# Two-layer encoder trunk on one core: the large loads move from SyncE's DMA queue to ScalarE's, and the planner gets two queues

## The chip, the cores and the metric

One core of one Trainium2 chip. The metric is device time in microseconds of one execution; lower is better. Before the change it is 1849.16 us, the median of three runs (1848.88 to 1854.86).

## What is computed

Two token groups (512 and 1024 rows, D = 1024) go through the same two layers. Cut to what matters:

```python
def even_layer(x, ...):                       # layer 0
    h = rms_norm(x, norm_g)
    qa, ka, va, qb, kb, vb, gate = split(h @ w_in)
    oa = gqa_attention(rope(norm(qa)), rope(norm(ka)), va)          # "A": 8 heads
    ob = diff_attention(rope(norm(qb)), rope(norm(kb)), vb, lam)    # "B": 4 heads, p0 - lam * p1
    mix = concat(oa, norm(ob)) * silu(gate)
    return x + mix @ w_out

def odd_layer(x, ...):                        # layer 1
    q, k, v, gate = split(rms_norm(x, norm_g) @ w_in)
    o = dilated_attention(q, k, v)            # "C": three (window, dilation) patterns, 16 heads
    return x + (o * silu(gate)) @ w_out
```

## The kernel before

**Precision by splitting.** Every matmul of a projection, of probabilities with V, and of the output is done in fp16 on split operands: ScalarE writes the high half (`f_hi`), VectorE the rest (`f_lo`), and TensorE makes three passes (`PASSES`, line 35). So each piece of data runs through ScalarE, VectorE, a transposing DMA and TensorE.

**Order of the work.** The program is cut into stages (`Plan.add`, line 66). A stage has an engine, a duration that the author estimates, dependencies, and buffers ("tokens") that it takes and gives back. `Plan.run` (line 96) plays the stages against these durations as a list scheduler: each engine takes the first stage by position whose inputs are ready and whose buffers are free, and emits its instructions there and then. So the durations decide the order in which instructions stand on each engine; on the chip every engine then runs its own list in order and waits at semaphores.

**DMAs in the planner.** `Plan.dma` (line 85) makes three stages of a transfer: an issue on SP (0.6 us for an ordinary one), a stage on one shared "DMA" server that works first come first served, and a latency. `tdma` (line 92) does it for a transposing DMA: with 2048 columns SP is taken for 0.05 + 2048 x 0.975e-3 us in the plan. All DMAs are issued from SP (`nc.sync`).

**What is loaded.** Large loads are 512 KB tiles of f32: two gain vectors (`norm_gain`, line 301), 12 token tiles in layer 0 (`l0_h`, line 1539), 74 blocks of weights (`wprep`, line 415: two for each pair of column blocks), and in `out_tile` for each of 24 output tiles the gated mix (line 1269) and the residual (lines 1302, 1306, 1307, 1309; 26 issues, as the first tile of each group in layer 1 takes two). These are 138 issues. Most of them land in the six f32 buffers `f4`, which attention uses as well for its exponentials.

**What is transposed.** `transp` (line 359, called from `t_av` and `out_tile`) turns a [128, 2048] fp16 tile of probabilities or of the mix; line 386 does it for the normalised tokens `hT`; line 594 turns queries and keys (1024 columns). TensorE's products with V (line 784) and the output projections (line 492 with `t`) cannot start before the transposed tile has landed.

**Stages in time.** Start and first projections to about 110 us; attention A with its projections to 450; B to 760; output of layer 0 and first projections of layer 1 to 1010; C to 1690; output of layer 1 to the end.

Of the kernel before, what the change touches and what calls it, by code (L numbers as in the profile page):

```python
# [20 lines left out]
D = 1024  # L21
# [20 lines left out]
LAG = {"PE": 0.25, "SP": 0.0, "DMA": 0.0, "LAT": 0.05, "ACT": 0.2, "DVE": 0.15, "POOL": 0.17}  # L42
LAT0 = 0.75


class Stage:
    def __init__(self, eng, dur, fn, pos, seq):
        self.eng, self.dur, self.fn, self.pos, self.seq = eng, dur, fn, pos, seq
        self.nd, self.succ, self.acq, self.rel = 0, [], [], []
        self.ready, self.done = 0.0, None  # L50
# [9 lines left out]
class Plan:  # L60
    def __init__(self, caps):
        self.caps = dict(caps)
        self.stages = []
        self.pos = 0.0

# [19 lines left out]
    def dma(self, issue, dur, fn, deps=(), acq=(), use=(), pos=None, keep=0, tail=1.25):  # L85


        a = self.add("SP", issue, fn, deps, acq, use, pos, keep)
        x = self.add("DMA", dur, None, [a], (), tuple(acq) + tuple(use), pos)
        return self.add("LAT", tail, None, [x], (), tuple(acq) + tuple(use), pos)  # L90

    def tdma(self, cols, *args, **kw):

        return self.dma(0.05 + cols * 0.975e-3, cols * 0.9e-3, *args, tail=1.2 + cols * 0.25e-3, **kw)

    def run(self):
# [17 lines left out]
        while n < len(self.stages):  # L114
            progress = False
            for e, q in engs.items():
# [24 lines left out]
                heapq.heappush(events, (now + s.dur, 1, s.seq, s))  # L141
                if e == "SP":
                    heapq.heappush(events, (now + LAT0, 2, s.seq, s))
# [8 lines left out]
            while events and events[0][0] <= now + 1e-9:  # L152
                t, kind, _, s = heapq.heappop(events)
                if kind == 0:
                    heapq.heappush(engs[s.eng], (t if s.eng == "DMA" else s.pos, s.seq, s))
                elif kind == 2:
                    release(s, t)
                else:
                    busy[s.eng] = False
                    s.done = t  # L160
                    for tok in s.rel:
                        tok.users -= 1
                        if tok.users == 0:
                            free[tok.kind].append(tok.slot)
                    if s.eng != "SP":
                        release(s, t)
# [3 lines left out]
def pe(n, cnt):  # L170
    return cnt * (n / 2400.0 + 0.0027)
# [34 lines left out]
T_ROW = dict(dur=1.3, tail=1.9)  # L206
T_COL = dict(dur=1.75, tail=1.9)
# [6 lines left out]
def trunk_kernel(ctx: ExitStack, tc: tile.TileContext, A: dict, outs: list):  # L214
    nc = tc.nc
# [76 lines left out]
    def norm_gain(l, deps=()):  # L292
# [5 lines left out]
        def f_ld():  # L298
            v = new(tok).rearrange("p a b c -> p (a b c)")
            b["g"], b["junk"] = v[:, 0:2048].bitcast(F32), v[:, 2048:3072].bitcast(BF16)  # L300
            nc.sync.dma_start(out=b["g"], in_=A[f"norm{l}"].unsqueeze(0).to_broadcast([128, D]))
# [97 lines left out]
    def wprep(w, cols, ih=None, iz=None, kinds=("whl",), deps=(), keep=2):  # L399
# [117 lines left out]
    def qk_stages(zb, ztok, evs, e2, tabs, tdep, ti, kind, isq, dst, dst_acq, dst_use, swap, dst_dep=()):  # L517
# [43 lines left out]
        else:  # L561
# [19 lines left out]
            s = add("DVE", dve(512) + 2 * dve(64) + 2 * dve(128) + 0.3 + (dve(384) if isq else 0.0), f_rope, [sr, tdep], [s1t],  # L581
# [484 lines left out]
    def att_C(u, gi):  # L1066
# [73 lines left out]
        def send():  # L1140
# [4 lines left out]
            s = add("ACT", act(512) + 0.12, f_ev, avs23[-1:], [pkt], [ot23])  # L1145
# [115 lines left out]
    def out_tile(l, g, tl, wo, mix_deps, x_deps, finish):  # L1261
# [36 lines left out]
        def f_x():  # L1298
            x = b["x"] = new(xt)
            if l == 0:  # L1300
                src = A["x_prompt"] if g == 0 else A["x_sample"]
                nc.sync.dma_start(out=x, in_=src[0, 128 * tl:128 * tl + 128, :])
            else:
                base = GROWS[g]
                if tl == 0:
                    nc.sync.dma_start(out=x[0:64, :], in_=x1buf[base + n - 64:base + n, :])
                    nc.sync.dma_start(out=x[64:128, :], in_=x1buf[base:base + 64, :])
                else:
                    nc.sync.dma_start(out=x, in_=x1buf[row - 64:row + 64, :])
        sx = dma(ISSUE, fn=f_x, deps=[x_deps, sl], acq=[xt], keep=1, **T_ROW)  # L1310
        evs, mms = [], []
        for hf in range(2):
# [21 lines left out]
            evs.append(add("DVE", 2 * dve(256) + 0.25, f_ev, [m, sx, evs], (), [pt, xt]))  # L1334
# [191 lines left out]
    def l0_h(g, tls, kinds):  # L1526
# [4 lines left out]
        for i, tl in enumerate(tls):  # L1531
            t1t = Token("t1")

            def f_ld(i=i, tl=tl):
# [4 lines left out]
                nc.sync.dma_start(out=b[i], in_=src[0, 128 * tl:128 * tl + 128, :])  # L1539
# [177 lines left out]
```

## Time and profile before

| | us |
|---|---|
| median of three runs | 1849.16 |
| the profiled execution's own time | 1854.62 |
| span in its trace (first to last instruction) | 1852.4 |
| TensorE (PE) busy | 1675.0 |
| VectorE (DVE) busy | 1332.2 |
| ScalarE (ACT) busy | 1212.8 |
| GpSimd (POOL) busy | 695.5 |

TensorE is busy in 90% of the span, so the time that it idles is the first thing to look at. Issues of DMAs are not in the busy times: SP has no busy time on the page, and an issue on another engine would show as idle time of that engine. How long SP is held by an issue stands in the timeline, in rows that begin with SPq.

### The profile page before, as it was taken

Reading aid. Unit: us, or ns where it says so; the run is one execution under the profiler, and the core shown is the slowest. Engines: PE = TensorE matmul, PEld = TensorE weight load, DVE = VectorE, ACT = ScalarE, POOL = GpSimd, SP = SyncE. Lnnn points to the kernel's source line nnn. Section 1 sums busy time; section 2 is a strip of 40 time slices with the busy share of each in tenths; the row PEclk is TensorE's granted clock in tenths of the full one; section 3 lists DMA queues with packets and bytes.
Section 4 is the critical chain, followed back from the end, with each engine's and each line's share of the span. In section 5 each row is a group of like instructions: output and inputs, shape, how many; then the busy total and the mean of one; then the engine's idle time right before and its main releaser. Section 6 shows DMA issues by size and latency. Waiting matters only on the chain. (4 is left out here: it accounts for less than half of the span.)

```text
span 1852.4 us, 44798 instructions
## 1 busy us (share of the span) xinstructions
PE 1675.0 (90%) x17626; PEld 1398.4 (75%) x17626; DVE 1332.2 (72%) x2985; ACT 1212.8 (65%) x2593; POOL 695.5 (38%) x1204
## 2 busy tenths in 40 slices
PE   4898978989999999699898999999999999995898
PEld 3776756878887878378787887888788888774788
DVE  7788878767888778965635778677777777787332
ACT  6488978767777767853425676678676757777220
POOL 6523333333463445312212344354444444452200
PEclk9999999999999999799899999999999999996999
DMA  9989999795565445689975676676766757776983
GB/s 251 191 157 166 182 177 167 146 163 113 98 125 101 109 92 122 147 198 224 207 176 128 122 150 131 138 143 140 147 132 144 137 116 151 148 145 140 232 230 103
DMA packets 788724, 282.06 MB, mean 152 GB/s; under 512 B 647072, under 2 KB 772256, under 8 KB 788512
## 3 DMA queue, kind: packets, MB, share of 16 engines
q1 hardware_dynamic: 788512, 279.19, 73.4%
q8 instruction: 138, 2.26, 0.5%
q14 instruction: 74, 0.61, 0.1%
HBM read 73.92 MB, written 25.17 MB: 53 GB/s over the span
## 5 line engine op out<-in xcount | busy, mean ns | idle before, releaser
L492 PE MATMUL pj<-whl,hT 128*128 128x256 f16 x7680 | 882.3, 275 | 22.2 <-DMA hT<-h 21.2
L492 PEld LDWEIGHTS <-hT 128*128 128x128 f16 x7968 | 782.8, 99 | 145.6 <-DMA hT<-h 23.1
L784 PEld LDWEIGHTS <-t 128*128 128x128 f16 x4992 | 200.5, 100 | 93.8 <-DMA t<-h 85.8
L1107 ACT ACTIVATE f<-f,cs,csc 128x256 f32<-128x256 f32 (+1 forms) x384 | 218.4, 570 | 65.5 <-DVE cs L778 65.4
L492 PEld LDWEIGHTS <-t 128*128 128x128 f16 x2304 | 228.9, 100 | 40.0 <-DMA t<-h 9.8
L800 DVE TENSOR_TENSOR h<-f,h 128x1024 f16<-128x1024 f32 x148 | 187.7, 1273 | 57.4 <-ACT h L796 55.0
L784 PE MATMUL pj<-V,t 128*128 128x64 f16 (+1 forms) x4032 | 178.7, 204 | 51.2 <-DMA t<-h 47.8
L492 PE MATMUL pj<-whl,t 128*128 128x256 f16 x1728 | 202.4, 279 | 8.2 <-DMA t<-h 8.2
L772 PE MATMUL S<-K,q 128*128 128x512 f16 x640 | 169.6, 399 | 33.3 <-ACT f L1024 19.1
L796 ACT ACTIVATE h<-f 128x1024 f16<-128x1024 f32 x168 | 175.5, 1051 | 21.9 <-DMA t<-h 19.8
L535 POOL TENSOR_SCALAR qs<-qs,we 128x8 f32<-128x8 f32 x87 | 44.5, 511 | 354.0 <-DVE qs L529 343.1
L261 POOL TENSOR_TENSOR qs<-qs,mhalf 128x8 f32<-128x8 f32 x87 | 147.8, 1699 | 7.3
L772 PEld LDWEIGHTS <-q 128*128 128x128 f16 x640 | 61.0, 101 | 91.7 <-issue 42.8
L854 DVE TENSOR_REDUCE as<-S 128x1 f32<-128x1024 f32 (+1 forms) x80 | 95.9, 1219 | 29.1 <-PE S L772 28.9
L423 ACT ACTIVATE t<-f 128x1024 bf16<-128x1024 f32 x74 | 77.8, 1051 | 44.5 <-DMA f<-in_w_in_dram 32.6
L864 ACT ACTIVATE f<-S,as,asc 128x1024 f32<-128x1024 f32 (+1 forms) x96 | 101.7, 1061 | 4.0 <-DVE h L800 0.5
L478 DVE SCALAR_TENSOR_TENSOR whl<-f,wsm,whl 128x1024 f16<-128x1024 f32 x68 | 87.7, 1305 | 8.2 <-ACT whl L473 8.2
L1332 DVE SCALAR_TENSOR_TENSOR f<-pj,os,f 128x256 f32<-128x256 f32 x96 | 41.9, 479 | 68.0 <-PE pj L492 61.2
L1018 DVE TENSOR_REDUCE bs<-S 128x1 f32<-128x1024 f32 x64 | 77.2, 1217 | 16.2 <-PE S L772 16.2
L800 POOL TENSOR_TENSOR h<-f,h 128x1024 f16<-128x1024 f32 x20 | 43.5, 2175 | 120.9 <-ACT h L796 120.9
L473 ACT ACTIVATE whl<-f,wsm 128x1024 f16<-128x1024 f32 x68 | 75.8, 1140 | 16.8 <-PE pj L492 14.3
L1122 PE MATMUL S<-K,q 128*128 128x256 f16 (+1 forms) x384 | 79.3, 371 | 4.6 <-DVE m L1097 4.6
(250 smaller groups left out, 2684.5 us busy)
## 6 DMA issues: line engine op xcount, KB each, us to landing
f<-in_w_in_dram SPq DMA_DIRECT2D x58, 512.0 KB, 5.3
mixbuf<-sg SPq DMA_DIRECT2D x48, 256.0 KB, 2.8
f<-mixbuf SPq DMA_DIRECT2D x24, 512.0 KB, 5.7
K<-K SPq DMA_DIRECT2D x78, 128.0 KB, 2.5
f<-in_w_out_dram SPq DMA_DIRECT2D x16, 512.0 KB, 4.5
pn<-pk SPq DMA_DIRECT2D x96, 66.0 KB, 2.2
x1buf<-f SPq DMA_DIRECT2D x12, 512.0 KB, 4.1
Vc<-V SPq DMA_DIRECT2D x96, 64.0 KB, 2.3
```

What stands on the lines that cost most here:

```text
L261: G.tensor_tensor(y, v, mhalf[:, 0:n], ALU.pow)
L423: S_.activation(out=junk1(t1t), in_=b[i].rearrange("p k n -> p (k n)"), func=AF.Square, accum_out=b["s"][:, i:i + 1])
L478: stt(out=part(k, 1, i), in0=b[i][:, nk * k:nk * k + nk, :], scalar=sc(), in1=part(k, 0, i), op0=M, op1=SU)
L492: T.matmul(ps, lhs(k, a), wt(k, b), start=(k == 0 and i == 0), stop=(k == 7 and i == 2))
L772: T.matmul(out[:, 512 * i:512 * i + 512], q, u.K[:, st, gi, hk, :], start=(st == 0), stop=(st == 1))
L784: T.matmul(o, t4[:, 8 * a + base + k, :], v(k, b), start=(k == 0 and i == 0), stop=(k == nk - 1 and i == 2))
L796: S_.activation(out=b["hl"][:, 0, :], in_=b["e"], func=AF.Copy)
L800: (G if on_pool else V).tensor_tensor(b["hl"][:, 1, :], b["e"], b["hl"][:, 0, :], SU)
L854: V.tensor_reduce(out=b["s"][:, 0:nh], in_=b["S"].rearrange("p (h k) -> p h k", h=nh), op=ALU.max, axis=AX.X)
L864: S_.activation(out=b["e"][:, w * i:w * i + w], in_=b["S"][:, w * i:w * i + w], func=AF.Exp, bias=b["s"][:, 2 + i:3 + i], scale=u.sc, accu ...
L1107: S_.activation(out=b["e"][:, w * i:w * i + w], in_=b["e"][:, w * i:w * i + w], func=AF.Exp, bias=b["s"][:, i:i + 1], scale=u.sc, accum_ou ...
L1122: T.matmul(s[:, L * i:L * i + L], q, k, start=(sk == 0), stop=(sk == 1))
```

## The change

The 138 loads named above are issued from ScalarE (`nc.scalar.dma_start`). Everything else stays on SP: transposing DMAs, the swapped copies of K (lines 599, 600), Vc, pn, the spills of the mix, the stores of results, and the small tables.

The planner learns of it. A transfer is now an issue on its own queue ("SP" or "ACT") and a landing that `transfer` works out when the issue is placed. For each queue it keeps when its last transfer was served and landed. An ordinary issue holds its engine for 0.6 us. A transposing one holds it for 0.6 + 0.64e-3 us per column, or until what is ahead of it on the same queue has nearly landed, whichever is longer. Transfers of the two queues don't delay each other in this model. Some durations are raised: matmuls by 2%, a rotary stage of queries by 0.25, the eviction of an output tile by 0.25, the copy of a C tile by 0.28 us.

```diff
-LAG = {"PE": 0.25, "SP": 0.0, "DMA": 0.0, "LAT": 0.05, "ACT": 0.2, "DVE": 0.15, "POOL": 0.17}
+LAG = {"PE": 0.25, "SP": 0.0, "LAT": 0.05, "ACT": 0.2, "DVE": 0.15, "POOL": 0.17}
...
+        self.served, self.landed = {"SP": 0.0, "ACT": 0.0}, {"SP": 0.0, "ACT": 0.0}
...
-    def dma(self, issue, dur, fn, deps=(), acq=(), use=(), pos=None, keep=0, tail=1.25):
-        a = self.add("SP", issue, fn, deps, acq, use, pos, keep)
-        x = self.add("DMA", dur, None, [a], (), tuple(acq) + tuple(use), pos)
-        return self.add("LAT", tail, None, [x], (), tuple(acq) + tuple(use), pos)
+    def dma(self, issue, dur, fn, deps=(), acq=(), use=(), pos=None, keep=0, tail=1.25, cols=0, queue="SP"):
+        a = self.add(queue, issue, fn, deps, acq, use, pos, keep)
+        a.move = (cols, dur, tail)
+        return self.add("LAT", 0.0, None, [a], (), tuple(acq) + tuple(use), pos)
 
     def tdma(self, cols, *args, **kw):
-        return self.dma(0.05 + cols * 0.975e-3, cols * 0.9e-3, *args, tail=1.2 + cols * 0.25e-3, **kw)
+        return self.dma(0.6 + cols * 0.64e-3, 0.0, *args, cols=cols, **kw)
+
+    def transfer(self, s, now):
+        cols, dur, tail = s.move
+        e, hold = s.eng, s.dur
+        if cols:
+            ahead = self.landed[e] - now
+            hold = max(s.dur, 0.95 * ahead if cols > 1024 else ahead - 0.8)
+            self.landed[e] = max(now + hold + 1.3 + cols * 0.5e-3, self.landed[e] + cols * 0.85e-3)
+            self.served[e] = self.landed[e] - 1.5
+        else:
+            self.served[e] = max(now + LAT0, self.served[e]) + dur
+            self.landed[e] = max(self.served[e] + tail, self.landed[e] + 0.15)
+        return hold, self.landed[e]
...
-    return cnt * (n / 2400.0 + 0.0027)
+    return cnt * (n / 2400.0 + 0.0027) * 1.02
...
-T_ROW = dict(dur=1.3, tail=1.9)
-T_COL = dict(dur=1.75, tail=1.9)
+T_ROW = dict(dur=1.3, tail=1.9, queue="ACT")
+T_COL = dict(dur=1.75, tail=1.9, queue="ACT")
...
-                nc.sync.dma_start(out=b[i], in_=w[:, c0:c0 + 128].rearrange("(k p) n -> p k n", p=128))
+                nc.scalar.dma_start(out=b[i], in_=w[:, c0:c0 + 128].rearrange("(k p) n -> p k n", p=128))
...
-            nc.sync.dma_start(out=b["mt"], in_=mixbuf[l][row:row + 128, :])
+            nc.scalar.dma_start(out=b["mt"], in_=mixbuf[l][row:row + 128, :])
```

The other loads are changed in the same way. Lines after the new code stand 18 further down in the changed kernel (`transp` is 377, the load of weights 433). In the rows below, t40, f42 and h41 are buffers of `t4` (transposed tiles), `f4` and `h4` (split tiles), with a running number.

**SP in attention A.** This is a piece of SP's list before, in the second head pair of A, where three loads of weights stand within 18 rows (here the first two, `f42` and `f45`):

```order
L415 DMA f42_2272<-in_w_in0_dram 128x8x128
L359 DMA_TRANSPOSE t42_2276<-h42_2227 128x16x128
L594 DMA_TRANSPOSE q1_2333<-st1_2266 128x8x128
L359 DMA_TRANSPOSE t40_2342<-h40_2270 128x16x128
L359 DMA_TRANSPOSE t41_2383<-h41_2335 128x16x128
L415 DMA f45_2442<-in_w_in0_dram 128x8x128
L359 DMA_TRANSPOSE t42_2449<-h42_2385 128x16x128
L359 DMA_TRANSPOSE t40_2519<-h40_2475 128x16x128
```

The same place of SP's list in the changed kernel, around the key and query of the same head pair:

```order
L377 DMA_TRANSPOSE t41_2223<-h41_2151 128x16x128
L612 DMA_TRANSPOSE q1_2240<-st1_2225 128x8x128
L377 DMA_TRANSPOSE t42_2282<-h42_2227 128x16x128
L377 DMA_TRANSPOSE t40_2343<-h40_2267 128x16x128
L377 DMA_TRANSPOSE t41_2374<-h41_2310 128x16x128
L377 DMA_TRANSPOSE t42_2440<-h42_2376 128x16x128
L377 DMA_TRANSPOSE t40_2476<-h40_2412 128x16x128
```

And ScalarE's list there in the changed kernel; L882 is an exponential of scores, L814 the high half of a tile of probabilities:

```order
L751 ACTIVATE z0_2402<-pj3_2196 128x2x2x64
L761 ACTIVATE sg1_2410<-pj3_2196,hz_1527 128x256
L814 ACTIVATE h40_2412<-f43_2370 128x1024
L433 DMA f40_2466<-in_w_in0_dram 128x8x128
L433 DMA f41_2468<-in_w_in0_dram 128x8x128
L793 ACTIVATE as_2438<-as_2438,ln14_78,ansc_435 128x2
L882 ACTIVATE f44_2471,den_2312<-S0_2404,as_2438,asc_434 128x512 x2
L814 ACTIVATE h41_2502<-f44_2471 128x1024
```

The loads have left the row of transposing issues on SP, and stand between a high half and the next exponential on ScalarE.

**ScalarE at the start.** ScalarE's first rows before; L1545 is the sum of squares of a token tile, L423 that of a block of weights:

```order
L1545 ACT_TABLE_LOAD
L1545 ACTIVATE t10_116,hs4_115<-f40_87 128x1024
L423 ACTIVATE t11_128,wsm_126<-f41_89 128x1024
L423 ACTIVATE t10_130,wsm_126<-f42_91 128x1024
L1545 ACTIVATE t11_136,hs4_135<-f43_93 128x1024
L378 ACTIVATE h40_146<-f40_87 128x1024
```

The end of the first ten loads, and what follows, on ScalarE in the changed kernel, with the semaphores that each row waits for (DMAHW0 is the semaphore of the first load, DMAHW1 of the second):

```order
L1557 DMA f44_95<-in_x_prompt_dram 128x1024
L1557 DMA f45_97<-in_x_prompt_dram 128x1024
L1557 DMA t40_99<-in_x_sample_dram 128x1024
L1557 DMA t41_113<-in_x_sample_dram 128x1024 [waits DMAHW0_49]
L1557 DMA t42_115<-in_x_sample_dram 128x1024 [waits DMAHW1_49]
L1563 ACT_TABLE_LOAD
L1563 ACTIVATE t10_118,hs4_117<-f40_87 128x1024
L441 ACTIVATE t11_128,wsm_126<-f41_89 128x1024 [waits DMAHW2_49]
```

Ten issues, the last two with a wait for a landing, now stand ahead of ScalarE's first activation, and none stands ahead of the first transposing issue on SP.

## Rows read from the trace of the kernel before

**Rows 1.** The page, first line and part 1: busy us, share, instructions.

```profile
span 1852.4 us, 44798 instructions
...
PE 1675.0 (90%) x17626; PEld 1398.4 (75%) x17626; DVE 1332.2 (72%) x2985; ACT 1212.8 (65%) x2593; POOL 695.5 (38%) x1204
```

**Rows 2.** Busy time by stretch: PE, PEld, DVE, ACT, POOL; PEclk, DMA share, GB/s.

```profile
0.00:75.00 75.00, 44.84 (x350) 36.69 (x351) 54.68 (x95) 45.45 (x74) 43.86 (x69) 0.95 1.02 243
...
110.00:450.00 340.00, 301.85 (x3720) 235.54 (x3719) 274.17 (x373) 270.27 (x475) 118.74 (x143) 0.96 0.90 164
...
760.00:1010.00 250.00, 218.52 (x1954) 185.18 (x1952) 146.09 (x306) 120.65 (x210) 57.06 (x151) 0.92 0.84 190
1010.00:1690.00 680.00, 638.58 (x7240) 549.33 (x7237) 511.17 (x1548) 479.46 (x1223) 304.06 (x519) 0.98 0.69 138
1690.00:1853.00 163.00, 144.41 (x1372) 125.45 (x1372) 62.08 (x174) 45.87 (x89) 12.80 (x22) 0.92 0.73 178
```

**Rows 3.** Waits of PE, whole span: us in total, times, longest us.

```profile
PE pj L784 <- DMA t<-h: 57.1, 53, 4.4
PE pj L435 <- ACT t L423: 21.2, 6, 11.5
PE pj L492 <- DMA hT<-h: 21.2, 9, 10.2
PE S L772 <- ACT f L1024: 19.1, 12, 3.8
PE S L772 <- ACT f L864: 10.6, 8, 2.3
```

**Rows 4.** Waits of PE in attention A, 110 to 450 us.

```profile
PE pj L784 <- DMA t<-h: 26.8, 24, 2.5
```

**Rows 5.** Timeline of SP, 165 to 215 us: start, us, what, how many.

```profile
165.19 5.53 SPq L359 DMA_TRANSPOSE t<-h  x2
170.77 0.58 SPq L415 DMA_DIRECT2D f<-in_w_in_dram  x1
171.51 3.70 SPq L359 DMA_TRANSPOSE t<-h  x1
...
197.13 4.57 SPq L359 DMA_TRANSPOSE t<-h  x2
...
213.50 3.95 SPq L359 DMA_TRANSPOSE t<-h  x1
```

**Rows 6.** Transposing issues of line 359, whole span: ns min/median/max.

```profile
L359 SPq DMA_TRANSPOSE t<-h x232: 1317/2098/7694, 105.4 to 1816.3; - x116
```

**Rows 7.** Loads of weights, 110 to 450 us: ns min/median/max.

```profile
L415 SPq DMA_DIRECT2D f<-in_w_in_dram x11: 572/599/1237, 122.5 to 442.1; - x11
```

**Rows 8.** Waits of PE in attention C, 1010 to 1690 us.

```profile
PE pj L784 <- DMA t<-h: 20.6, 20, 4.4
```

**Rows 9.** Loads of input weights, 1010 to 1690 us.

```profile
L415 SPq DMA_DIRECT2D f<-in_w_in_dram x20: 573/588/1817, 1063.2 to 1481.5; - x20
```

**Rows 10.** Timeline of all engines at the start: start, us, what, idle before.

```profile
6.46 1.06 ACT L1545 ACTIVATE t<-f 128x1024 bf16<-128x1024 f32 x1 [4.46 <-DMA f<-in_x_prompt_dram]
...
7.56 1.38 SPq L1539 DMA_DIRECT2D t<-in_x_sample_dram  x3
...
15.78 4.42 SPq L386 DMA_TRANSPOSE hT<-h  x1
...
22.25 4.57 PE L492 MATMUL pj<-whl,hT 128*128 128x256 f16 x24 [10.20 <-DMA hT<-h]
```

**Rows 11.** Waits of PE, 760 to 1010 us.

```profile
PE pj L784 <- DMA t<-h: 4.9, 3, 2.1
PE pj L492 <- DMA t<-h: 1.9, 2, 1.0
```

**Rows 12.** Waits of PE, 1690 us to the end.

```profile
PE pj L492 <- DMA t<-h: 6.3, 3, 2.5
PE pj L784 <- DMA t<-h: 3.3, 3, 1.5
```

More of the change, by code (lines that the diff above doesn't have):

```diff
@@ L49, in __init__ @@
         self.nd, self.succ, self.acq, self.rel = 0, [], [], []
-        self.ready, self.done = 0.0, None
+        self.ready, self.done, self.move = 0.0, None, None
 class Token:
@@ L140, in run @@
                 busy[e] = e != "LAT"
-                heapq.heappush(events, (now + s.dur, 1, s.seq, s))
-                if e == "SP":
-                    heapq.heappush(events, (now + LAT0, 2, s.seq, s))
+                hold = s.dur
+                if s.move is not None:
+                    hold, t = self.transfer(s, now)
+                    heapq.heappush(events, (t, 2, s.seq, s))
+                heapq.heappush(events, (now + hold, 1, s.seq, s))
                 n += 1
@@ L154, in run @@
                 if kind == 0:
-                    heapq.heappush(engs[s.eng], (t if s.eng == "DMA" else s.pos, s.seq, s))
+                    heapq.heappush(engs[s.eng], (s.pos, s.seq, s))
                 elif kind == 2:
@@ L164, in run @@
                             free[tok.kind].append(tok.slot)
-                    if s.eng != "SP":
+                    if s.move is None:
                         release(s, t)
@@ L1301, in f_x @@
                 src = A["x_prompt"] if g == 0 else A["x_sample"]
-                nc.sync.dma_start(out=x, in_=src[0, 128 * tl:128 * tl + 128, :])
+                nc.scalar.dma_start(out=x, in_=src[0, 128 * tl:128 * tl + 128, :])
             else:
@@ L1305, in f_x @@
                 if tl == 0:
-                    nc.sync.dma_start(out=x[0:64, :], in_=x1buf[base + n - 64:base + n, :])
-                    nc.sync.dma_start(out=x[64:128, :], in_=x1buf[base:base + 64, :])
+                    nc.scalar.dma_start(out=x[0:64, :], in_=x1buf[base + n - 64:base + n, :])
+                    nc.scalar.dma_start(out=x[64:128, :], in_=x1buf[base:base + 64, :])
                 else:
-                    nc.sync.dma_start(out=x, in_=x1buf[row - 64:row + 64, :])
+                    nc.scalar.dma_start(out=x, in_=x1buf[row - 64:row + 64, :])
         sx = dma(ISSUE, fn=f_x, deps=[x_deps, sl], acq=[xt], keep=1, **T_ROW)
@@ L1333, in f_ev @@
                         in1=b["x"][:, cs], op0=M, op1=AD)
-            evs.append(add("DVE", 2 * dve(256) + 0.25, f_ev, [m, sx, evs], (), [pt, xt]))
+            evs.append(add("DVE", 2 * dve(256) + 0.5, f_ev, [m, sx, evs], (), [pt, xt]))
         finish(g, tl, lambda: b["x"], evs, xt)
@@ L1538, in f_ld @@
                 src = A["x_prompt"] if g == 0 else A["x_sample"]
-                nc.sync.dma_start(out=b[i], in_=src[0, 128 * tl:128 * tl + 128, :])
+                nc.scalar.dma_start(out=b[i], in_=src[0, 128 * tl:128 * tl + 128, :])
             ld = dma(ISSUE, fn=f_ld, acq=[xts[i]], **T_ROW)
```

6 lines of the change are left out of this document (3 added, 3 removed).

## The prediction, made before the changed kernel was run

> **What bounds the kernel now.** I read the page first: PE is busy in 1675.0 of 1852.4 us [rows 1], so the most that can be won by feeding PE better is the 177 us in which it stands idle. The busy time by stretch then says where those lie [rows 2]: 75.00 - 44.84 = 30.2 us at the start, 340.00 - 301.85 = 38.2 in attention A, 31.5 between the layers, 41.4 in C, 18.6 at the end. The list of PE's waits says for whom [rows 3]: 57.1 us in 53 waits for a transposed tile of probabilities or mix (`t<-h` at line 784), 21.2 for transposed tokens (`hT<-h`), and 21.2 + 19.1 + 10.6 = 50.9 for ScalarE in its three largest groups. With the output projections' own waits, 1.9 and 6.3 us [rows 11, 12], some 86 of the 177 us end with a transposing DMA. That is what this change works on.
>
> Why those tiles come late is seen in SP's timeline in attention A [rows 5]. From 165.19 to 217.45 us SP has 15 rows, with 46 us of issues in 52: a transposing issue holds SP for about 2.3 us when nothing but transposes is around it (197.13: two in 4.57 us), and SP is nearly full. Behind a load the same issue holds SP for 3.70 us (171.51) and 3.95 us (213.50), after 0.58 us for the load itself (170.77). Over the whole kernel the median hold is 2.098 us and the longest 7.694 [rows 6]. So a load costs SP its 0.6 us and, where a transpose follows, another 1.4 to 1.8 us in which that transpose waits for the load to be served; every tile behind is as much later.
>
> **What the change removes, adds and moves.** 138 load issues leave SP and stand on ScalarE. Nothing is computed that was not computed before, and the same bytes move. Five terms follow.
>
> *Attention A.* Eleven loads of weights are issued there [rows 7]. Each gives SP back 0.6 us and, by the holds above (3.70 and 3.95 against 2.3), about 1.4 us of the next transpose: 11 x 2.0 = 22 us of SP time. PE waits 26.8 us for transposed tiles there [rows 4]. SP is full in parts of this stage only, so I take half: -11 us. The ends are 0, if the tile is late all the same because load and transpose share the DMA engines, and -22.
>
> *Attention C.* Twenty loads of input weights [rows 9], and transposes that stand further apart; PE waits 20.6 us for transposed tiles [rows 8]. The same price would be 20 x 2.0 = 40 us of an SP queue with more room in it. I take a third of PE's waits, -6 us; the ends are 0 and -20.6.
>
> *The start.* PE's first projection waits 10.20 us, until 22.25, for a transpose whose issue at 15.78 was held 4.42 us [rows 10]; with no load ahead, 2.1 us would do, so it gains 2.3. But ScalarE now issues the first ten loads itself. On SP the tenth had ended at 7.56 + 1.38 = 8.94 us, and ScalarE's first sum of squares stood at 6.46 us: it can't stand before 8.94 plus the table load now, some 3 us later, and its next steps make up a part of that, since they too had waited for loads. The two nearly cancel for the first tile; the seven tiles behind it gain. I take -2 us, with ends of +4 and -8.
>
> *Between the layers and at the end.* PE's waits for transposed tiles are 4.9 + 1.9 us [rows 11] and 6.3 + 3.3 us [rows 12], 16.4 in all; loads are densest here, and ScalarE is least busy (120.65 of 250 us, 45.87 of 163 [rows 2]), so that its issues are covered. I take a quarter, -4 us; ends 0 and -12.
>
> *The price on ScalarE.* No row shows an issue on ScalarE. The nearest is the same load on SP, 0.588 to 0.599 us at the median [rows 7, 9]: 138 x 0.59 = 81 us on an engine that is busy for 1212.8 of 1852.4 us [rows 1]. ScalarE has 640 us of room, and PE waits for it for 50.9 us in the groups of rows 3. If these waits grow as ScalarE's load does (81 / 1213 = 7%), that is 3.4 us; I take +5, as an issue also delays what stands behind it. The lower end is 0, if issues fall into ScalarE's own waits; the upper one is +25, about a third of the 81 us, if they fall on the path in A, where ScalarE is busy for 270.27 of 340 us [rows 2], and in C.
>
> *The new order of everything.* The plan's durations change, so all engines' lists differ in detail. The old plan gave every 2048-column transpose 2.05 us of SP, whatever stood ahead; the rows show 1.3 to 7.7 [rows 6]. The new one has 1.91 us or the wait for what is ahead on the queue, which is nearer. I take 0 here, with 6 us either way.
>
> The sum is -11 - 6 - 2 - 4 + 5 = -18 us: 1854.6 - 18 = 1836.6 against the profiled execution's own time, which is 5.5 us above the median of the runs. Against the median 1849.2 it is **1831 us**.
>
> A rule speaks against this sum. The Trainium skill, in "DMA: Bandwidth & Descriptors", section "Issuing engines are not separate DMA queues", says that DMAs of all issuing engines run on the same 16 DMA engines and interleave, so that a second issuing engine saves only the time that it takes to initiate them. By it a transpose would land as late as before, and the terms above would shrink to what 0.6 us an issue is worth. The holds in rows 5 speak for more: a queue's issue that waits for what is ahead of it is time of SP's list and not of the DMA engines; whether the transfer behind it is any faster, no row shows yet.
>
> **Rivals.** *Nothing won (0.17).* A load that starts with a transpose takes its share of the DMA engines from it. In A the DMA share is 0.90 of the stretch, at the start 1.02 [rows 2], which speaks for this; in C, 0.69, against it. The 1.4 us of hold then come back as a later landing, SP's gain is 0.6 us a load, which pays for ScalarE's 0.59: 1843 to 1855, about 1848.
>
> *ScalarE becomes the late one (0.25): slower.* In the changed list a load waits on ScalarE for its buffer and for an earlier DMA's semaphore, as the ninth and tenth at the start do, and all of ScalarE's exponentials and high halves stand behind it. It may also be held while SP's transposing issue is served. The transposes of line 359 alone hold SP for 232 x 2.1 = 487 us, 26% of the span [rows 6]; in rows 5 transposes hold it for most of the time. If a load meets one in 43% of cases, between the two, and loses half a hold, 1.05 us, each time, ScalarE's price is 138 x (0.59 + 0.45) = 144 us rather than 81. It decides once ScalarE's delay is on PE's path for more than a fifth of that, 29 us, since the gains were 23 and may be half of it: +29 - 12 = +17, about 1866 us; the case reaches from 1855 to 1885. For it: PE already waits for ScalarE about as long as for `t<-h`. Against it: 640 us of idle ScalarE.
>
> The Trainium skill's "Perfetto Trace Analysis", section "DMA Instruction — HWDGE (DVE, Sync)", describes the mechanism that such a hold would have: the descriptor generator is shared by the issuing sequencers, is locked by one of them, and the lock's wait is part of the issue's profiled time. No run here shows it so far, as only one engine issues.
>
> *A larger gain (0.14).* The new plan fits the queue so well that half of the 86 us of waits for transposes go, and ScalarE's price is hidden: 1849 - 43 + 5 = 1811 us; 1800 to 1818. For it: the waits are many and short (53 of 57.1 us, none over 4.4 [rows 3]), so a small shift clears many. Against it: C has 20 loads of input weights in 680 us [rows 2, 9], so most of its waits have other causes.
>
> That the loads don't move can be left out: they stand on ScalarE in its list.
>
> **How the numbers follow.** The forecast, 1818 to 1843 us, has a chance of 0.44; the larger gain 0.14; nothing won 0.17; ScalarE late 0.25. About 0.3%, 5.5 us, is what a measurement here can tell from no change. Faster by more is the forecast, the larger gain and 0.03 of "nothing won": 0.61. Within it is the rest of that case, 0.14. Slower is 0.25. The range reaches from 1806, inside the larger gain, to 1863, inside the slower case, and leaves out about 0.07 below and 0.13 above.
>
> **What would show it right or wrong.** Right: in the timeline of SP no hold over about 3 us for transposes of line 377 in A; PE's waits for `t<-h` in A down from 26.8 to 15 or so, in C from 20.6 to about 14; issues of about 0.6 us in ScalarE's rows; the first projection still near 22 us. The sharing rival shows as holds back at 2.1 us while times to landing stay; the slower one as ScalarE issues well over 0.6 us, and PE's waits for ScalarE up by more than 20 us. Wrong altogether would be a change of time that lies in stretches without loads, and so comes from the new order alone.

## The result: slower by 5.4%, and the profile of the changed kernel

The changed kernel takes 1954.17 us at the median (1940.62 to 1958.16), beside 1850.41 (1848.88 to 1854.86) for the kernel before on the same chip: a ratio of 1.0544, with a 95% interval of 1.0489 to 1.0598. That is some 100 us slower, outside the range that was forecast (1806 to 1863), and beyond every rival.

The page of the changed kernel, its first line, part 1 and the two large queues of part 3 (packets, MB, share of 16 engines; q1 is SP's queue, q10 ScalarE's):

```profile
span 1950.8 us, 44821 instructions
...
PE 1685.6 (86%) x17626; PEld 1405.2 (72%) x17626; DVE 1333.2 (68%) x2985; ACT 1211.1 (62%) x2593; POOL 689.3 (35%) x1204
...
q1 hardware_dynamic: 702592, 207.88, 58.2%
q10 hardware_dynamic: 85920, 71.31, 13.3%
```

The engines do the same work as before: against [rows 1], DVE, ACT and POOL are within 7 us, PE 10.6 us longer. The span is 98.4 us longer, so PE idles 88 us more. Its waits say for whom:

```profile
PE pj L802 <- DMA t<-h: 124.2, 66, 11.7
PE pj L510 <- DMA t<-h: 18.7, 8, 5.4
PE S L790 <- ACT f L1042: 18.0, 13, 4.3
...
PE pj L453 <- ACT t L441: 13.6, 1, 13.6
...
PE S L790 <- ACT f L882: 10.5, 9, 4.2
```

The wait for transposed tiles at the product with V (line 802, 784 before) is 124.2 us where it was 57.1, and its longest single wait 11.7 where it was 4.4 [rows 3]; at the output projections (line 510) it is 18.7, after 1.9 + 6.3 [rows 11, 12]. That is 67.1 + 10.5 = 77.6 of the 88 us. ScalarE's three groups of rows 3 are now 18.0 + 13.6 + 10.5 = 42.1 us, below the 50.9 of before; with the smaller groups PE waits for ScalarE 67.1 us, after 66.7.

The same waits in stretches of the changed kernel: the first row is of 110 to 450 us, the next two of 760 to 1010, the fourth of 1010 to 1690, the last two of 1690 to the end.

```profile
PE pj L802 <- DMA t<-h: 37.5, 27, 4.7
...
PE pj L510 <- DMA t<-h: 13.0, 4, 5.4
PE pj L802 <- DMA t<-h: 9.7, 5, 3.3
...
PE pj L802 <- DMA t<-h: 30.9, 17, 5.4
...
PE pj L802 <- DMA t<-h: 29.4, 7, 11.7
...
PE pj L510 <- DMA t<-h: 5.7, 4, 2.2
```

Every stretch from which a gain was forecast has lost: A 26.8 to 37.5 [rows 4], C 20.6 to 30.9 [rows 8], between the layers 6.8 to 22.7 [rows 11], the end 9.6 to 35.1 [rows 12]. (The stages end later in the changed kernel, the last product with V 88 us later, so a part of the last row is still C; C and the end together go from 30.2 to 66.0.)

Holds and landings, by line: the transposing issues of line 377, their landings, and the loads of weights on ScalarE (ns min/median/max; landings in us).

```profile
L377 SPq DMA_TRANSPOSE t<-h x232: 1317/2087/15128, 111.4 to 1914.7; - x116
...
DMA to landing us min/median/max: 4.2/4.8/17.1
...
L433 ACTq DMA_DIRECT2D f<-in_w_in_dram x58: 373/385/1543, 1.6 to 1561.8; - x58
```

The landings of the transposing issues in the kernel before (line 359):

```profile
DMA to landing us min/median/max: 4.2/4.8/9.6
```

The median hold is 2.087 us after 2.098 [rows 6], the median landing 4.8 us before and after. Only the tail has grown: the longest hold from 7.694 to 15.128 us, the longest landing from 9.6 to 17.1. An issue on ScalarE costs 0.385 us, less than the 0.59 assumed.

**One of the long ones.** At 1811.89 us a transposing issue starts on SP; on ScalarE a load of the gated mix was issued 1.6 us before it and a second one 1.0 us behind it. (SP itself had issued two stores of results just before.) The timelines of SP, ScalarE and PE there (start, us, what, idle before):

```profile
1811.89 4.83 SPq L377 DMA_TRANSPOSE t<-h  x1
...
1810.28 0.33 ACTq L1287 DMA_DIRECT2D f<-mixbuf  x1
...
1812.85 0.36 ACTq L1287 DMA_DIRECT2D f<-mixbuf  x1
...
1813.49 0.86 PE L802 MATMUL pj<-Vc,t 128*128 128x64 f16 x24
...
1828.68 1.46 PE L802 MATMUL pj<-Vc,t 128*128 128x64 f16 x24 [11.70 <-DMA t<-h]
```

The busy time in 1815 to 1828 us (us, PE, PEld, DVE, ACT, POOL, PEclk, DMA share, GB/s):

```profile
1815.00:1828.00 13.00, 1.98 (x19) 1.53 (x16) 1.49 (x6) 0.00 (x0) 4.18 (x8) 0.78 1.26 96
```

And the packets of SP's queue in the same 13 us (count, MB, share of 16 engines):

```profile
q1 hardware_dynamic: 2600, 0.73, 100.2%
```

PE runs out of work and waits 11.70 us. The DMA engines have packets under way all the time (their times add up to 1.26 of what 16 engines have) and move only 96 GB/s: the times of 2600 packets of SP's queue are 100.2% of 16 engines' 13 us, which is 208.4 / 2600 = 0.080 us a packet. So it is no lack of work for the DMA engines: the transfers of both queues crawl. The transpose lands 16.7 us after its issue, and the load behind it 15.6 us.

Such a wait costs more than its length. The granted clock stood at the lower of its two levels, 1.2 GHz (0.50), for a while after PE had run out of work (the columns are those of the stretch above):

```profile
1822.20:1832.40 10.20, 3.72 (x36) 3.05 (x37) 1.22 (x5) 3.03 (x6) 0.00 (x0) 0.50 1.09 102
```

Twenty-four matmuls of line 802 took 0.86 us at 1813.49 and take 1.46 us at 1828.68. Over the whole kernel the mean granted clock is 0.947, after 0.959 before; PE's 10.6 us more of busy time go with it.

### The profile page after: what moved, and what is told of

It is laid out like the page before. It is cut to its first block, busy times and chain, and to the rows that moved or that the text cites. A ratio compares the mean times of both kernels' runs of the same rounds, so it can differ in the third digit from the quotient of the medians.

```text
span 1950.8 us, 44821 instructions
## 1 busy us (share of the span) xinstructions
PE 1685.6 (86%) x17626; PEld 1405.2 (72%) x17626; DVE 1333.2 (68%) x2985; ACT 1211.1 (62%) x2593; POOL 689.3 (35%) x1204
## 4 chain that ended last, share of the span: by engine, by line
PE 29%; DMA 12%; DVE 5%; POOL 3%; ACT 1%; issue 1%; SPq 0%; DVEq 0%; ACTq 0%; POOLq 0%
PE pj L510 23%; DMA t<-h 9%; PE pj L802 2%; DMA Vc<-V 1%; DVE f L1115 1%; PE S L1140 1%; PE pj L524 1%; PE S L1188 1%; POOL qs L279 1%; DMA pn<-pk 1%; ACT f L1125 1%; DVE h L818 1%; DMA x1buf<-f 0%; POOL pn L1254 0%; POOL sg L1255 0%
## 5 line engine op out<-in xcount | busy, mean ns | idle before, releaser
L510 PE MATMUL pj<-whl,t 128*128 128x256 f16 x1728 | 204.0, 280 | 18.8 <-DMA t<-h 18.7
L814 ACT ACTIVATE h<-f 128x1024 f16<-128x1024 f32 x168 | 175.1, 1051 | 31.5 <-DMA t<-h 29.4
L553 POOL TENSOR_SCALAR qs<-qs,we 128x8 f32<-128x8 f32 x87 | 39.8, 457 | 425.1 <-DVE qs L547 403.2
L279 POOL TENSOR_TENSOR qs<-qs,mhalf 128x8 f32<-128x8 f32 x87 | 153.1, 1760 | 7.2
L882 ACT ACTIVATE f<-S,as,asc 128x1024 f32<-128x1024 f32 (+1 forms) x96 | 101.6, 1060 | 4.7 <-DVE h L818 1.3
L604 ACT ACTIVATE st<-t 128x512 f16<-128x512 f32 x87 | 54.0, 621 | 58.4 <-DVE t L598 32.9
L608 DVE TENSOR_TENSOR st<-t,st 128x512 f16<-128x512 f32 x87 | 60.7, 697 | 41.6 <-ACT st L604 41.4
L672 ACT ACTIVATE z<-pj 128x256 f32<-128x256 f32 x78 | 29.3, 376 | 95.5 <-PE pj L510 89.2
```

What stands on the lines that cost most here:

```text
L279: G.tensor_tensor(y, v, mhalf[:, 0:n], ALU.pow)
L510: T.matmul(ps, lhs(k, a), wt(k, b), start=(k == 0 and i == 0), stop=(k == 7 and i == 2))
L814: S_.activation(out=b["hl"][:, 0, :], in_=b["e"], func=AF.Copy)
L882: S_.activation(out=b["e"][:, w * i:w * i + w], in_=b["S"][:, w * i:w * i + w], func=AF.Exp, bias=b["s"][:, 2 + i:3 + i], scale=u.sc, accu ...
```

## The experiments

The theory after this profile: a load on the other queue still delays a transpose, and worse than one ahead of it on its own queue (sharing). Rivals: ScalarE is late because it issues; or the loss is of the new order of instructions and not of the queue at all. Ratios are to the kernel before on the same chip.

### The queue alone, the plan alone, and a plan that takes the queues as one

**Before's order, the 138 loads on ScalarE** (planner as before; the edit at one of the places):

```diff
-                nc.sync.dma_start(out=b[i], in_=w[:, c0:c0 + 128].rearrange("(k p) n -> p k n", p=128))
+                nc.scalar.dma_start(out=b[i], in_=w[:, c0:c0 + 128].rearrange("(k p) n -> p k n", p=128))
```

> The order of the kernel before, its planner untouched; only the 138 loads are issued from ScalarE, at the places that the old plan had given them on SP. Theory S (a load in flight on the other queue delays a transposing DMA as much as one ahead on its own, and a load issued during a transpose delays it further): slower than before, 1880 to 1930 us, with PE's waits for t<-h over 90 us. Theory P (the new plan's order is what is bad, the queue is harmless): 1835 to 1860. Theory A (ScalarE is late, since issues and their waits stand in its list): 1880 to 1930 too, but with PE's waits for ScalarE up by 20 us or more and those for t<-h as before.

Measured: 1904.03 us, 1.0288 [1.0244, 1.0333]. With not one instruction in another place on its engine's list except the loads, the queue costs 53 us. The first two waits of PE:

```profile
PE pj L784 <- DMA t<-h: 103.1, 50, 12.8
PE pj L435 <- ACT t L423: 25.2, 5, 13.3
```

The waits for transposed tiles grow by 46 us, those for ScalarE hardly (53.9 us in the three groups, after 50.9). So it is the transposes again. Which of them come late can be counted in the two traces. The 232 transposing issues of line 359 are sorted by the 138 loads around them: a load is ahead when it was issued before the transposing issue and lands after its start, and behind when it is issued between that start and the transpose's landing. Medians in us:

| loads | on SP: count, hold, landing | on ScalarE: count, hold, landing |
|---|---|---|
| none | 142, 1.96, 4.50 | 138, 1.93, 4.48 |
| ahead | 35, 3.58, 5.78 | 35, 3.68, 5.85 |
| behind | 33, 1.96, 4.59 | 33, 2.20, 5.85 |
| ahead and behind | 22, 3.56, 5.95 | 26, 3.70, 7.57 |

A load ahead costs nearly the same on either queue at the median, in the hold and to the landing. What the second queue adds is the price of a load behind, and most of all of loads on both sides (at the longest 17.99 us to the landing, after 8.33).

**The change's planner, all loads on SP:**

```diff
-T_ROW = dict(dur=1.3, tail=1.9, queue="ACT")
-T_COL = dict(dur=1.75, tail=1.9, queue="ACT")
+T_ROW = dict(dur=1.3, tail=1.9, queue="SP")
+T_COL = dict(dur=1.75, tail=1.9, queue="SP")
```

> The new planner with its durations and its rule for transposing issues, but all loads planned on and issued from SP. Theory S: 1835 to 1865 us, as before or a little better. Theory P: 1920 or more, since the durations and the rule alone would do the harm. Theory A: as S.

Measured: 1892.19 us, 1.0233 [1.0192, 1.0273]. A miss: the plan is not harmless. It costs 43 us with no load moved, and the queue adds 58 to that (1.0544 - 1.0233 = 3.1%).

**The change, with a planner that puts both queues into one account:**

```diff
-        e, hold = s.eng, s.dur
+        e, hold = "SP", s.dur
```

> Loads on ScalarE's queue as in the changed kernel, but the plan keeps one landing time for both queues, so that a transposing issue is planned to wait for a load on the other queue. Theory S with half of the loss from a plan that doesn't know of the delay: 1880 to 1920 us. If the loss is physical alone: 1940 to 1960. Theory A: 1940 to 1960, ScalarE's issues are as many.

Measured: 1901.93 us, 1.0281 [1.0244, 1.0319]. Half of the loss comes back by one line: what the planner believes of the queues is worth some 50 us.

**The change, with small loads.** 74 loads of weights and 24 of the gated mix move 64 KB and repeat it over the tile (the edit for the weights; the 40 other loads stay at 512 KB):

```diff
-                nc.scalar.dma_start(out=b[i], in_=w[:, c0:c0 + 128].rearrange("(k p) n -> p k n", p=128))
+                nc.scalar.dma_start(out=v[:, 0:1, :], in_=w[0:128, c0:c0 + 128].rearrange("(k p) n -> p k n", p=128))
+                b[i] = v[:, 0:1, :].to_broadcast([128, 8, 128])
```

> The changed kernel in which the 74 loads of weights and the 24 of the mix move 64 KB in place of 512 (the first 128 columns, read eight times over; the results are those of other weights). Same plan, same issues on ScalarE at the same places. Theory S: transposes are hardly delayed, 1840 to 1880 us, PE's waits for t<-h back to some 60 us. Theories A and P: 1935 to 1960, nothing on ScalarE or in the order has changed.

Measured: 1858.76 us, 1.0047 [1.0026, 1.0067]. The same issues stand on ScalarE at the same places; with an eighth of the bytes nearly all of the loss is gone. ScalarE's issuing is not the main cause; the bytes are. (Smaller loads gain on one queue too; a pair below tells how much.)

### Which part of the plan

**Before's rule and queue, with the four raised durations:**

```diff
-    return cnt * (n / 2400.0 + 0.0027)
+    return cnt * (n / 2400.0 + 0.0027) * 1.02
...
-            s = add("ACT", act(512) + 0.12, f_ev, avs23[-1:], [pkt], [ot23])
+            s = add("ACT", act(512) + 0.4, f_ev, avs23[-1:], [pkt], [ot23])
```

> The kernel before with the four raised durations alone (matmuls by 2%, three evictions and rotary stages by 0.25 to 0.28 us); old rule for DMAs, loads on SP. Theory R (the new rule for transposing issues and landings does the plan's harm): 1840 to 1860 us. Theory D (the durations do it): 1880 to 1900. Theory N (any new order loses, since the order before is the best of many tries): 1860 to 1900 here, and in each other re-planned run.

Measured: 1868.74 us, 1.0096 [1.006, 1.0131], which of the three ranges only "any new order loses" had; the next run speaks against that.

**The new rule with the old durations, loads on SP** (the second run with the four durations put back):

```diff
-    return cnt * (n / 2400.0 + 0.0027) * 1.02
+    return cnt * (n / 2400.0 + 0.0027)
```

> The new rule for DMAs with the old durations, all loads on SP. Theory R: 1880 to 1900 us, as with both. Theory D: 1840 to 1860. Theory N: 1860 to 1900.

Measured: 1830.04 us, 0.9896 [0.9865, 0.9927]: faster than both kernels, and below every range that was expected. PE's wait for transposed tiles at line 802 is 49.3 us.

**Before with matmuls 0.5% longer in its plan**, as a measure of what any small edit does:

```diff
+    return cnt * (n / 2400.0 + 0.0027) * 1.005
```

> The kernel before with planned matmuls 0.5% longer, a change far below what the plan's durations can be off by; it only shuffles the order. Theories R and D: 1840 to 1858 us. Theory N: 1860 or more.

Measured: 1856.89 us, 1.0031 [1.001, 1.0053], so about 6 us.

**Before's order, loads on ScalarE, small loads** (the first and the fourth edit together):

> The old plan with the loads issued from ScalarE, and the 74 loads of weights and the 24 of the mix 64 KB in place of 512 (first 128 columns read eight times over; other results). Theory S (bytes of loads in flight beside transposes): 1815 to 1855 us, PE's waits for t<-h near 50 us. If the loss is in issuing from ScalarE, with the same issues at the same places: 1885 to 1910.

Measured: 1826.33 us, 0.9884 [0.9846, 0.9921]. In before's order too the loss goes with the bytes. How much of that is the queue's price, the next run tells.

### The pairs that were missing

**Before's order, small loads on SP:** the same edit with `nc.sync`.

> The order of the kernel before, all loads still on SP, but the 74 loads of weights and the 24 of the gated mix move 64 KB in place of 512 KB (each reads one eighth of its columns, and the tile repeats it, so the values are not the reference's). The pair with the run that has the same order and the same small loads on ScalarE (1826.3 us) gives what the queue alone does once the bytes are small. Sharing (a load delays transposes by its bytes, on whichever queue): the bytes go here too, and SP keeps its 98 issues of 0.59 us, which the forecast priced at 0.6 us each on a queue that is full in parts: 1832 to 1846 us, 6 to 20 us above the other. Rival (ScalarE's queue has a gain of its own, as the forecast had it, about 2 us a load in A and C): 1846 us or more. Rival (an issue is worth nothing on either engine): 1822 to 1830.

Measured: 1813.93 us, 0.9818 [0.9776, 0.9859]: a miss, below every range that was expected, and faster than with the small loads on ScalarE by 0.7%. So the small loads by themselves gain 1.8%, and the queue's price falls with the bytes from 2.9% to 0.7%, with 40 large loads still on ScalarE. The forecast had ScalarE's queue as a gain; there is none, even here. The Trainium skill's "DMA: Bandwidth & Descriptors", section "Issuing engines are not separate DMA queues", allows a second issuing engine only the time of initiating. This pair shows not even that, and with loads of 512 KB the queue costs 2.9%.

**The change without the raised durations** (new rule, loads on ScalarE):

> The change without its four raised durations: new rule, loads on ScalarE's queue. The pair with the new rule and old durations on SP (1830.0 us) gives the price of the queue within another order than before's. Sharing: the price comes again, 40 to 75 us, and somewhat more than in the old order (53.7 us), since this plan believes that the queues don't delay each other: 1870 to 1905 us; PE's waits for transposed tiles of probabilities and mix above 90 us. Rival (the loss belongs to the raised durations and the particular order, and the queue is harmless where the rule is right): 1822 to 1840.

Measured: 1919.73 us, 1.0381 [1.0327, 1.0435]. Against 0.9896 for the same plan on SP the queue costs 4.9%, 90 us, more than was expected. How much of it comes from a plan that takes the queues as independent, the run with one account below tells.

**The new rule on SP with the matmuls' 2% alone:**

> The new rule, loads on SP, old durations but for the matmuls' 2%. Between 1830.0 us (no raised duration) and 1892.2 us (all four). If the plan is made worse by believing PE slower (it then places transposes later than PE wants them): most of the 62 us, 1870 to 1895. If the other three carry it: 1825 to 1845. If the order is only sensitive, so that any small edit moves the time by 10 to 30 us with no system: anywhere between, 1840 to 1870 the likeliest.

Measured: 1884.09 us, 1.0196 [1.0152, 1.0239]: of the four durations it is the matmuls' that hurts.

**The new rule with one account for both queues, old durations, loads on ScalarE:**

> Loads on ScalarE's queue, old durations, and the planner takes the two queues as one (a transpose is held until loads of either queue have nearly landed). Between the new rule on SP (1830.0 us) and the same loads on ScalarE with the planner's two queues (the run beside this one). Sharing with a planner that is wrong about it: a good part of the queue's price comes back, 1845 to 1880. Rival (the plan's belief is worth nothing, the transfers themselves cost it all): as the run with two queues, within 10 us.

Measured: 1885.58 us, 1.0219 [1.0165, 1.0273], slightly above what was expected. A third of the queue's 90 us comes back; the rest is there with this account too.

### Transposes beside loads, alone

**Pairs and streams.** A kernel of its own, run once, with eight rounds of each pair: `hl` is a tile of zeros, VectorE's small operations are to hold every pair back until the one before has landed, and `pause` is a VectorE pass of 0.7 us.

```python
for i, t, f in pair("tfront", "ffront", "T", "L", 1):   # transpose first, load one pass later
    nc.sync.dma_start_transpose(out=t, in_=hl)
    nc.scalar.dma_start(out=f, in_=row(i))
```

> The disputed cost by itself: this kernel leaves out the whole computation and issues transposes of 2048 columns (4 KB a partition) and loads of 512 KB, eight of each arrangement, each pair waiting for the pair before: a transpose alone; a load alone (rows of 4 KB, or pieces of 512 bytes as for weights); both on SP's queue, the load ahead; load on ScalarE and transpose on SP together; the load one VectorE pass (about 1 us) ahead; the transpose one pass or three ahead; then 16 transposes in a row alone, with 16 loads between them on SP, and with 16 loads on ScalarE. Sharing (loads on the other queue delay a transpose all the same): alone a hold near 2.0 us and a landing near 4.4; on one queue 3.5 and 5.7; with the load on ScalarE together or ahead a hold of 2.5 to 3.7 and a landing of 5.5 to 7; with the transpose ahead a hold near 2.0 but a landing of 6 us or more, which one queue never shows; 16 transposes with loads on ScalarE end at least 20% later than with the same loads on SP. Rival (side by side they are harmless, and the kernel's loss has to do with what else it moves): landings within 1 us of 4.4 with the load on ScalarE, and the stream with loads on ScalarE ends no later than on SP.

The landings (operation, count, median us from issue to landing):

```profile
talone<-hl SPq DMA_TRANSPOSE x8, 4.3
...
tboth<-hl SPq DMA_TRANSPOSE x8, 5.6
tbehind<-hl SPq DMA_TRANSPOSE x8, 5.6
tfront<-hl SPq DMA_TRANSPOSE x8, 6.5
...
tbfront<-hl SPq DMA_TRANSPOSE x8, 6.8
tlate<-hl SPq DMA_TRANSPOSE x8, 4.4
```

Alone (`talone`) a transpose lands after 4.3 us. With a load of the other queue 0.9 us behind it (`tfront`, `tbfront` for weights) it takes 6.5 to 6.8, and with the load 2.4 us behind it (`tlate`) 4.4 again. That is the sharing, and it comes from a load that is issued later.

The pairs with ScalarE's load meant ahead did not become what they were meant to be. In `tboth` and `tbehind` nothing tied a load to the transposed tile of the round before, so from the third round on the next load was issued 0.2 us behind the transposing issue. In SP's and ScalarE's timelines:

```profile
207.20 1.78 SPq L121 DMA_TRANSPOSE tbehind<-hl  x1
...
207.40 0.34 ACTq L120 DMA_DIRECT2D fbehind<-in_x_sample_dram  x1
```

Their 5.6 us are those of a load close behind; what a load ahead on the other queue does to the hold, which was part of the expectation, these pairs don't show.

Three stretches of streams, of 16 transposes each: with ScalarE's loads, with SP's, and alone (us, DVE, POOL, PEclk, DMA share, GB/s):

```profile
468.40:543.60 75.20, 1.01 (x6) 0.00 (x0) 1.00 1.12 233
...
544.00:615.00 71.00, 1.17 (x7) 0.00 (x0) 1.00 1.06 236
615.00:659.00 44.00, 1.98 (x11) 0.00 (x0) 1.00 1.03 191
```

The packets in the last of them (count, MB, share):

```profile
q1 hardware_dynamic: 33280, 8.39, 103.0%
```

The landings in the first stretch, and in the second:

```profile
DMA to landing us min/median/max: 4.4/5.5/19.5
...
DMA to landing us min/median/max: 4.6/5.7/5.9
```

The streams were a miss, in two ways. Nothing kept ScalarE's 16 loads back, so they ran beside the 16 transposes that were meant to be alone, from 468.4 us, and the last 16 ran alone. And 16 transposes with 16 loads take 75 us on two queues and 71 on one, 6% more and not 20%. But single transposes land after up to 19.5 us beside the other queue's loads, and never after more than 5.9 on one queue. Undisturbed, a packet of a transpose takes 16 x 44 x 1.03 / 33280 = 0.022 us. The pairs explain some 2 us a transpose; the stream has landings as long as the kernel's, but doesn't show which order of transfers makes them.

**Load, transpose, load.** Loads stood on both sides of the transpose at 1811.89 us. A second kernel, run once, has that order alone, eight rounds of each case:

```python
case("one", "L T p L p p p T")     # L: load on ScalarE, T: transpose on SP, p: VectorE pass of 0.7 us
case("two", "L p T p L p p p T")
case("sp", "S T p S p p p T")      # S: the same load on SP
case("few", "L T L")
```

> Where a transpose of the changed kernel lands more than 10 us after its issue, loads of ScalarE's queue stand on both sides of it: one just ahead, so that the transpose is held, and one issued during the hold, with a second transpose behind. This kernel leaves out the computation and issues that pattern alone, eight times each: load, transpose, load (rows of 4 KB) and a second transpose, with the first load close ahead (one) or 0.7 us ahead (two); the same on SP's queue alone (sp); with weights' pieces of 512 bytes, one or two of them behind (wb, wbb); with a store ahead (st); two loads ahead and none behind (ahead); transpose, load, transpose (tl); and without the second transpose (few). If the pattern itself makes it: landings of 9 us or more for the transpose and the load behind it in one, two, wb, wbb or few, and none over 8 in sp, ahead and tl. Rival (the pair shares as in the earlier pairs, and the collapse needs something else that the kernel has at those moments): no landing over 8.5 us anywhere, 5.5 to 7.5 for the first transpose with loads on ScalarE, and sp within 1 us of that.

The landings of its cases, named by the case (`oneta` is the first transpose of `one`, `twob` the second load of `two`):

```profile
twob<-in_x_sample_dram ACTq DMA_DIRECT2D x8, 512.0 KB, 10.6
...
oneta<-h SPq DMA_TRANSPOSE x8, 9.0
...
twota<-h SPq DMA_TRANSPOSE x8, 11.7
twotb<-h SPq DMA_TRANSPOSE x8, 10.0
spta<-h SPq DMA_TRANSPOSE x8, 5.4
...
wbta<-h SPq DMA_TRANSPOSE x8, 7.3
...
aheadta<-h SPq DMA_TRANSPOSE x8, 7.2
...
tlta<-h SPq DMA_TRANSPOSE x8, 6.7
...
fewta<-h SPq DMA_TRANSPOSE x8, 10.6
```

The stretches of `one`, `two` and `sp` (columns as above):

```profile
7.00:107.00 100.00, 35.47 (x108) 0.00 (x0) 1.00 0.90 168
107.00:238.00 131.00, 41.29 (x116) 0.00 (x0) 1.00 1.00 128
238.00:330.00 92.00, 34.46 (x103) 0.00 (x0) 1.00 0.80 183
```

This is the changed kernel's collapse, with nothing else running. `sp` is `one` on a single queue: there the first transpose lands after 5.4 us, with the loads on ScalarE after 9.0, and eight rounds take 92 and 100 us. On one queue the second load's issue has to wait for SP, and stands over 3 us behind the transposing issue; on two it stands 0.9 us behind. With the first load 0.9 us ahead and not 0.2 (`two`) the transpose lands after 11.7 us and the load behind it after 10.6, and eight rounds take 131 us at 128 GB/s, of which the additional pass explains under 6. Three transfers are enough (`few`, 10.6). With the second load issued together with the transpose (`ahead`, 7.2), or none ahead (`tl`, 6.7), it stays under 8; with weights' pieces of 512 bytes it is milder (`wb`, 7.3, and 8.6 with two loads behind), below the 9 us that were expected. With a store ahead on SP it is 8.4, so the store at 1811.89 us is not needed for it.

`few` holds a second answer. Its holds, and those of the first transpose of `sp` (ns min/median/max):

```profile
L83 SPq DMA_TRANSPOSE fewta<-h x8: 1318/3511/3741, 784.2 to 864.8; - x8
...
L83 SPq DMA_TRANSPOSE spta<-h x8: 3024/3531/3764, 237.9 to 316.6; - x8
```

A transposing issue is held 3.5 us at the median behind a load of the other queue, as it is behind one of its own, and as the table of before's order has it in the kernel. (In two of the eight rounds of `few` it is held 1.3 us; in `sp` never.)

### Is the rule's gain its own

**The new rule on SP, matmuls 0.5% longer, and 2% shorter, in the plan:** `* 1.005` and `* 0.98` in the line shown above.

> The new rule on SP with old durations (1830.0 us, ratio 0.9896), matmuls 0.5% longer in the plan. If the rule's gain is of the rule: 1822 to 1842. If the order is only sensitive and that one was a lucky draw: 1840 to 1880.

> The same with matmuls 2% shorter in the plan, where 2% longer gave 1884.1 us. If the plan is hurt by believing PE slower than it is, going the other way does no such harm: 1815 to 1845. If any move by 2% away from the tuned durations costs the same: 1860 to 1890.

Measured: 1834.31 us, 0.9912 [0.989, 0.9933], and 1846.05 us, 0.9957 [0.9938, 0.9976]. The first is where it was expected, the second 1 us above its range. Both are below the kernel before, so the gain is not one lucky order; 2% shorter costs 11 us of it, where 2% longer cost 55 (1.0196 - 0.9896). Why the two sides differ so much was not found.

## Why the prediction was wrong

In ratios, the change is three things: the new rule on one queue, -1.0% (-19 us); the raised durations on top of it, +3.4% (+62 us); the queue on top of both, +3.1% (+58 us). Together +5.4%.

- **The step that failed is attention A's price, "about 1.4 us of the next transpose", with its ends of 0 and -22;** C, the start and the end rest on it too. It took the hold behind a load [rows 5] for a property of the queue. The hold stays when the load is on the other queue (3.68 us, after 3.58 on SP, in before's order; 3.511 and 3.531 alone), so only the 0.6 us of the issue could be won. And the ends left a loss out, with no reason that excluded it: on one queue a load issued behind a transpose hardly delays it (4.59 us to the landing, after 4.50 with no load near), and no row of before could show what a load on the other queue does there. That is 5.85 us in before's order with the loads on ScalarE, 6.5 after 4.3 for a pair, and 9.0 to 11.7 after 5.4 for load, transpose, load. The queue's terms were forecast as -23 us, -18 with ScalarE's price, and measured as +53 in before's order and +90 in the new rule's.
- **The start** was forecast as -2, with ends of +4 and -8; PE's waits up to 110 us grow from 33.3 to 39.4 us. The first projection stands at 22.07 us, as forecast near 22. The next transposed tile is what loses: SP's and PE's timelines of the changed kernel show the second transpose held for 8.14 us, and PE waiting for it. Two loads of weights were in flight on ScalarE's queue there, beside SP's own small tables, and two loads of tokens followed during the hold.

```profile
22.37 8.14 SPq L404 DMA_TRANSPOSE hT<-h  x1
...
36.22 4.02 PE L510 MATMUL pj<-whl,hT 128*128 128x256 f16 x18 [9.08 <-DMA hT<-h]
```

- **The price on ScalarE** was over-estimated: 0.33 to 0.39 us an issue at the median, and 66 us for all 138 with the few long ones, not 81; PE's waits for ScalarE stayed as they were in total (67.1 us, after 66.7). The slower rival had the right sign by the wrong mechanism. The Trainium skill's "Perfetto Trace Analysis", section "DMA Instruction — HWDGE (DVE, Sync)", has a wait for the lock of the descriptor generator within an issue's profiled time. This case shows none of a hold's length: 41 of the 138 issues on ScalarE began during a transposing issue of SP and took 0.37 us at the median, the other 97 took 0.38.
- **"Nothing won"** had the mechanism, sharing, but neither its sign nor its size. Its sign, holds back at 2.1 us and landings as before, did not come: behind a load the holds stay (3.68 us in before's order), and landings come later. It priced sharing as if two transfers that share lose nothing together, which nearly holds for the total of the stream (75 and 71 us) and not for the kernel, where both crawl at 96 GB/s.
- **The new order, "0 here, with 6 us either way",** was the second error: with all loads on SP it measured +43 us. Half a percent on the matmuls in before's plan moves 6 us, which is where such a term might stand; but the rule alone gave -19 us and the matmuls' 2% in its plan +55, and these were four different edits whose prices were put into one zero.
- What the text named as signs of being right did not come: in A holds of up to 6.5 us stayed, and the waits rose to 37.5 us rather than falling to 15.

The version to keep is the new rule with the old durations and all loads on SP: 1830.04 us, 0.9896 of the kernel before.

## What to carry to other kernels

A second DMA queue takes away an order as well as a wait: in one queue a transpose was hardly delayed by a load issued after it, and a transpose on the critical path should keep that protection. Where a hold behind a transfer looks like the queue's, ask whether it is the transfer's own, which another queue won't remove, and let the range reach to the other sign where the trace can't show the new overlap. Where a planner sets the order, its new rule, its new durations and the move itself are separate edits, each to be run alone.

## What the runs showed of the hardware

- A transposing issue waits for a load of the other queue as for its own: in the kernel a hold of 3.7 us beside 3.6, and 3.5 alone on either.
- A load issued behind a transpose delays it on two queues (landing 5.85 us in the kernel, after 4.48 with no load near) and hardly on one (4.59, after 4.50).
- Load, transpose, load on two queues, with rows of 4 KB: the DMA engines have packets under way while the rate falls, from 183 GB/s on one queue to 168 or 128, by the distance of the first load, and to 96 in the changed kernel. A packet of SP's queue takes 0.080 us there, and 0.022 in 16 transposes alone. What inside the DMA engines makes the packets slow, and why the stream, with landings of up to 19.5 us, loses only 4 us in its total, stays open.
- In the changed kernel the granted clock fell after PE's 11.70 us wait had begun: 0.50 from 1822 to 1832 us, with 1.46 us for matmuls that took 0.86.
